# The second token half's residual steps behind the first half's first eight blocks of h2

## The chip, the cores and the metric

The kernel runs on one core of one Trainium2 chip. The metric is the device time in microseconds (us). The engines are TensorE (PE; its weight loads are listed as PEld), VectorE (DVE), ScalarE (ACT), GpSimd (POOL) and SyncE (SP, which issues most loads).

## What is computed

One layer of a diffusion backbone over 256 latent tokens of width 2048, with 256 context tokens. The mixer (attention and a recurrent branch) ends in an output projection; then, in the reference:

```python
out_l = merge_branches(attn_l, hgo_l, hg_l[6], gl_l, hgrn_o_norm[layer],
                       w_br_mla[layer], w_br_hgrn[layer], w_out[layer])
x = x + gt_a * rmsnorm(out_l, norm_g[layer, 1])
h = modulate(rmsnorm(x, norm_g[layer, 2]), sh_f, sc_f)
x = x + gt_f * rmsnorm(swiglu(h, w_ffn_in[layer], w_ffn_out[layer]), norm_g[layer, 3])
```

The change lies between the output projection (`w_out`) and the first products of the feed-forward part (`w_ffn_in`). Everything is float32; each large product is made of three passes over operands that are split into a high part and a low part (high x high, low x high, high x low).

## The kernel before

Tokens are in two halves of 128 (`hf` 0 and 1), the width of 2048 in four chunks of 512 (`c`) or 16 of 128 (`k`).

The output projection runs `project_tok` four times, for four column chunks, with both halves in two PSUM tiles. In the fourth, the last products are ordered so that half 0 ends 12 products before half 1. ACT squares each result with a sum (line 860), DVE multiplies it by the gate row into `x1` (863), and after the fourth chunk `rstd_part` makes the factor `r1[hf]` of the norm (838 to 840).

The residual steps follow, for half 0 and then for half 1 in program order: four times a DVE step that forms `x1 * r1 + xr` (line 871) and an ACT square with a sum (873), then `rstd_part` for `rt2[hf]`.

Then h2, the normed and modulated input of the feed-forward part, is made transposed. For every half and chunk, DVE forms `xq` = `x1` x `rt2` x `A2b` (881), PE transposes it in four pieces into one PSUM bank (884), and for each of the four pieces ACT writes the high part (888, with the shift as bias) and DVE the low part (889: the same value less the high part). There are four such PSUM banks (pool `px`), eight `xq` buffers. The instructions of the last piece are kept in `h2[hf, c]`.

The first chunk of the feed-forward products (`first_chunk`) takes its weights in pieces of 1024 columns, two `k` each. `half` splits one piece: an ACT cast makes the high part (line 108), DVE the low part (110). The split of `k` 0 to 3 (`wf0`) was made before, behind the output projection. `products` runs three matmuls for each `k` and half (919): first `k` 0 to 9 for half 0, then the same for half 1, then the rest with the halves in turn. The third matmul of each `k` is the one that needs the low part of the weights. The splits go through three pairs of buffers. `mod_job` is a DVE reduction over another loaded tile that shares the load buffers. After the first chunk, `project_tok` (825) does all further feed-forward products.

The program is queued by the Tile scheduler, which takes, for each engine, what is ready in its own model of the time, and among that what was written earlier first. `issue_after` adds only an order: the instructions of its block on an engine are queued behind the named instruction of the same engine. In the kernel before, such orders put the first split behind block (0, 0) of h2 and the second and third behind block (0, 1). The residual steps of half 1 have none.

Of the kernel before, what the change touches and what calls it, by code (L numbers as in the profile page):

```python
# [7 lines left out]
F32 = mybir.dt.float32  # L8
F32R = mybir.dt.float32r
U32 = mybir.dt.uint32  # L10
AF = mybir.ActivationFunctionType
ALU = mybir.AluOpType
PSUM = bass.MemoryType.PSUM

P = 128
# [4 lines left out]
NFF = 44  # L20
# [6 lines left out]
def block_kernel(  # L27
# [20 lines left out]
    nc = tc.nc  # L48
# [3 lines left out]
    ap = ctx.enter_context(tc.tile_pool(name="ap", bufs=16))  # L52
# [3 lines left out]
    px = ctx.enter_context(tc.tile_pool(name="px", bufs=4, space=PSUM))  # L56
# [17 lines left out]
    ident = c0[:, 0:128]  # L74
# [23 lines left out]
    def load_w(src, cols=2048):  # L98
        raw = wp.tile([P, cols], F32, tag="raw", name="raw")
        last_load[0] = nc.sync.dma_start(raw, src)  # L100
        return raw

    def split_w(raw, cols=2048, tags=("wH", "wL"), step=1024, pool=wp, bufs=None):
        parts = []
        for o in range(0, cols, step):
            n = min(step, cols - o)
            H = pool.tile([P, n], F32R, tag=tags[0], name="wH", bufs=bufs)
            nc.scalar.copy(H, raw[:, o:o + n])  # L108
            L = pool.tile([P, n], F32R, tag=tags[1], name="wL", bufs=bufs)
            nc.vector.tensor_tensor(L, raw[:, o:o + n], H.bitcast(F32), op=ALU.subtract)  # L110
            parts.append((H, L))

        def get(o, n):
            H, L = parts[o // step]
            q = o % step
            return H[:, q:q + n], L[:, q:q + n]

        return get

    def split_into(raw, tiles):  # L120

        for i, (H, L) in enumerate(tiles):
            nc.scalar.copy(H, raw[:, i * 512:(i + 1) * 512])
            nc.vector.tensor_tensor(L, raw[:, i * 512:(i + 1) * 512], H.bitcast(F32), op=ALU.subtract)

        def get(o, n):
            return tuple(t[:, o % 512:o % 512 + n] for t in tiles[o // 512])

        return get

    def split_act(dst, src, heng=None):
        nc.scalar.copy(dst[:, 0, :], src)
        nc.vector.tensor_tensor(dst[:, 1, :], src, dst[:, 0, :].bitcast(F32), op=ALU.subtract)
# [38 lines left out]
    def wide(u):  # L172
        return u.rearrange("p e t -> p (e t)")
# [93 lines left out]
    for g, nk in enumerate(GROUPS + [0, 0]):  # L267
# [6 lines left out]
        for kt in range(nt):  # L274
            if nk:
# [4 lines left out]
                for kk in range(per):  # L280
                    k = kt * per + kk
                    nc.tensor.matmul(pm[32 * (k % 4):32 * (k % 4) + 32, 0:n], cst[:, k], raw[:, kk * n:(kk + 1) * n],  # L282
                                     start=(k < 4), stop=(k >= KD - 4))
# [14 lines left out]
        pt = px.tile([P, 512], F32, tag="px", name="pt")  # L298
        for i in range(2 * nk):
            nc.tensor.matmul(pt[:, 2 * i:2 * i + 2], row[:, i * P:(i + 1) * P], sel,  # L300
                             start=(i == 0), stop=(i == 2 * nk - 1))
# [5 lines left out]
                                       op0=ALU.add, op1=ALU.mult)  # L307
# [441 lines left out]
    units = [hx[:, 1, 8 + j] for j in range(8)] + [hx[:, 0, j] for j in range(8)]  # L749
    spare = [hx[:, 1, j] for j in range(8)] + [hx[:, 0, 8 + j] for j in range(8)]  # L750
    for j in range(KD):
# [4 lines left out]
        for br, src in enumerate(([aT[:, h] for h in range(NH)], hgT)):  # L756
            for k in range(NH):
                H, L = w(br * 1024 + k * P, P)
                for z, (l, r) in enumerate(((H, src[k][:, 0, :]), (H, src[k][:, 1, :]), (L, src[k][:, 0, :]))):
                    nc.tensor.matmul(ps[:, br * T:(br + 1) * T], l, r, start=(br == 0 and k == 0 and z == 0),  # L760
                                     stop=(br == 1 and k == NH - 1 and z == 2))
# [15 lines left out]
    SH2 = wk.tile([P, KD], F32, name="SH2")  # L777
# [11 lines left out]
    def rows(i, vec, tiles):  # L789
        pg = px.tile([P, 512], F32, tag="px", name="pg")  # L790
        nc.tensor.transpose(pg[0:KD, 0:P], vec, ident)
        grow = wk.tile([KD, P], F32, tag="scs", name="grow")
        nc.scalar.copy(grow, pg[0:KD, 0:P])
        nc.sync.dma_start(gdr[i], grow)
        for c, g in enumerate(tiles):
            nc.sync.dma_start(g, gdr[i, 4 * c:4 * c + 4].rearrange("k p -> (k p)").partition_broadcast(P))
        return tiles
# [37 lines left out]
    def rstd_part(i, hf):  # L835

        rt = wk.tile([P, 16], F32, name=f"rt{i}{hf}")[:, 0:1]
        nc.vector.tensor_reduce(rt, ssq[:, i, hf], axis=mybir.AxisListType.X, op=ALU.add)
        nc.scalar.activation(rt, rt, AF.Sqrt, bias=epst, scale=1.0 / D)
        nc.vector.reciprocal(rt, rt)  # L840
        return rt

    def pairs(tiles):
        return list(zip(tiles[0::2], tiles[1::2]))

    g1b = gate_rows(0, [ap.tile([P, 512], F32, tag="hC", name="gbc", bufs=8) for _ in range(4)])
    x1 = bp.tile([P, 2, D], F32, tag="b16", name="x1")
# [3 lines left out]
    A2b = rows(2, A2, [wk.tile([P, 512], F32, tag=t, name="A2b") for t in ("kt", "ktn", "vT", "vn")])  # L851
# [12 lines left out]
        if c == 0:  # L864
            sqrt_table(ssq[:, 0, 0, 0:1])
    wf0 = split_into(load_w(wfi[0, 0]), pairs([wide(u) for u in spare[8:]]))
    rt2 = []
    for hf in range(2):
        for c in range(4):
            cs = slice(c * 512, (c + 1) * 512)  # L870
            nc.vector.scalar_tensor_tensor(x1[:, hf, cs], x1[:, hf, cs], r1[hf], xr[:, hf, cs], op0=ALU.mult, op1=ALU.add)
            junk = wk.tile([P, 512], F32, tag=("f", "kk")[hf], name="junk")
            nc.scalar.activation(junk, x1[:, hf, cs], AF.Square, accum_out=ssq[:, 1, hf, c:c + 1])
        rt2.append(rstd_part(1, hf))

    h2 = {}
    for hf in range(2):
        ts_ = slice(hf * P, (hf + 1) * P)
        for c in range(4):
            xq = ap.tile([P, 512], F32, tag="hC", name="xq", bufs=8)  # L880
            nc.vector.scalar_tensor_tensor(xq, x1[:, hf, c * 512:(c + 1) * 512], rt2[hf], A2b[c], op0=ALU.mult, op1=ALU.mult)
            pt = px.tile([P, 4, P], F32, tag="px", name="pxt")
            for i in range(4):
                nc.tensor.matmul(pt[:, i], xq[:, i * P:(i + 1) * P], ident, is_transpose=True, start=(i == 0), stop=(i == 3))
            for i in range(4):
                j = 4 * c + i
                h = units[j]
                hi = nc.scalar.activation(h[:, 0, ts_], pt[:, i], AF.Identity, bias=SH2[:, j:j + 1], scale=1.0)
                lo = nc.vector.scalar_tensor_tensor(h[:, 1, ts_], pt[:, i], SH2[:, j:j + 1], h[:, 0, ts_].bitcast(F32),
                                                    op0=ALU.add, op1=ALU.subtract)  # L890
            h2[hf, c] = (hi, lo)


    G = [None] * NFF
    g_row = []

    def behind(ins):
        es = ExitStack()
        for i in ins:
            es.enter_context(tc.issue_after(i.ins))  # L900
        return es

    def first_chunk():

        ps = [pj.tile([P, 512], F32, tag="pj", name="pst") for _ in range(2)]
        raws = [load_w(wfi[0, 1]), load_w(wfi[0, 2])]
        ws = [lambda k: wf0(k * 512, 512)] * 4

        def half(raw, i):
            w = split_w(raw[:, i * 1024:(i + 1) * 1024], 1024)  # L910
            for kk in range(2):
                ws.append(lambda k, kk=kk: w(kk * 512, 512))

        def products(ks, hf):
            for k in ks:
                H, L = ws[k](k)
                aH, aL = (units[k][:, e, hf * P:(hf + 1) * P] for e in range(2))
                for n, (l, r) in enumerate(((aH, H), (aL, H), (aH, L))):
                    nc.tensor.matmul(ps[hf], l, r, start=(k == 0 and n == 0), stop=(k == KD - 1 and n == 2))  # L919

        with behind(h2[0, 0]):
            half(raws[0], 0)
        with behind(h2[0, 1]):
            half(raws[0], 1)
            half(raws[1], 0)
        products(range(0, 10), 0)
        products(range(0, 10), 1)
        half(raws[1], 1)
        raw = load_w(wfi[0, 3])
        half(raw, 0)  # L930
        half(raw, 1)
        for k in range(10, KD):
            for hf in range(2):
                products((k,), hf)
        return ps
# [18 lines left out]
    def turn(j):  # L954

        g = g_row[2 * j:]
        for b in range(0, 4, 2):
# [5 lines left out]
            for i in range(2):  # L963
                G[4 * j + b + i] = u = spare[(4 * j + b + i) % 16]
                split_act(u, pt[:, i])
# [4 lines left out]
    def ffn_out(part, hook):  # L970
        q0 = 4 * part
        nq = min(4, NFF // 4 - q0)
        for c in range(4):
            cs = slice(c * 512, (c + 1) * 512)
            ps = project_tok(lambda q: wfo[c, q0 + q], 4 * nq, lambda k: G[4 * q0 + k], part == 0, part == 2,
                             pairs([ap.tile([P, 512], F32R, tag="hC", name="wl", bufs=8) for _ in range(8)])
# [168 lines left out]
```

## Time and profile before

| | |
|---|---|
| Median of 3 runs | 1741.63 us (1738.98 to 1741.84) |
| Profiled execution | 1740.55 us, span 1738.8 us |
| PE busy | 1694.0 us, 97% of the span |
| DVE busy | 1089.0 us, 63% |
| ACT busy | 766.2 us, 44% |
| Mean granted clock of PE | 0.991 |

Times in rows count from the start of the span. A busy PE is not a PE at its peak, since matmuls overlap; how closely their starts follow each other tells more. A timeline row merges neighbouring instructions of one kind: start, length of the whole, engine, line, operation, output <- inputs, shape, count, and in brackets the idle time before it and what ended it. The granted clock is a share of 2.4 GHz.

### The profile page before, as it was taken

Reading aid. Unit: us, or ns where it says so; the run is one execution under the profiler, and the core shown is the slowest. Engines: PE = TensorE matmul, PEld = TensorE weight load, DVE = VectorE, ACT = ScalarE, POOL = GpSimd, SP = SyncE. Lnnn points to the kernel's source line nnn. Section 1 sums busy time; section 2 is a strip of 40 time slices with the busy share of each in tenths; the row PEclk is TensorE's granted clock in tenths of the full one; section 3 lists DMA queues with packets and bytes.
Section 4 is the critical chain, followed back from the end, with each engine's and each line's share of the span. In section 5 each row is a group of like instructions: output and inputs, shape, how many; then the busy total and the mean of one; then the engine's idle time right before and its main releaser. Section 6 shows DMA issues by size and latency. Waiting matters only on the chain.

```text
span 1738.8 us, 22134 instructions
## 1 busy us (share of the span) xinstructions
PE 1694.0 (97%) x8715; PEld 1410.4 (81%) x8715; DVE 1089.0 (63%) x1619; ACT 766.2 (44%) x1086; POOL 51.7 (3%) x81
## 2 busy tenths in 40 slices
PE   6898999999999999999999899999999999999997
PEld 4457888888888888889998788888888888888886
DVE  5335777777778766666765765664456655544456
ACT  5225443343345444445544554444444443344443
POOL 0100000000000000001210000000000000000000
PEclk9899999999999999999999999999999999999999
DMA  9983455655556565578766456665566665555653
GB/s 389 357 330 148 162 178 194 217 194 194 180 183 231 193 253 189 194 290 303 278 222 224 167 218 242 234 234 187 194 242 233 234 233 208 194 193 185 214 193 121
DMA packets 60247, 383.78 MB, mean 221 GB/s; under 512 B 7104, under 2 KB 7920, under 8 KB 16880
## 3 DMA queue, kind: packets, MB, share of 16 engines
q1 hardware_dynamic: 55328, 368.15, 58.1%
q0 software_dynamic: 4096, 13.11, 1.9%
q8 instruction: 68, 1.11, 0.3%
q10 hardware_dynamic: 720, 1.12, 0.2%
q14 instruction: 35, 0.29, 0.0%
HBM read 376.03 MB, written 6.32 MB: 220 GB/s over the span
## 4 chain that ended last, share of the span: by engine, by line
PE 94%; DMA 2%; DVE 2%; ACT 1%; issue 0%; SPq 0%; DVEq 0%; ACTq 0%
PE pst L825 45%; PE ps L144 13%; PE ps L148 11%; PE ps L149 5%; PE psb L760 5%; PE pre L144 3%; DMA raw<-in_wm_dram 2%; PE pm L282 1%; PE pst L919 1%; PE psS L698 1%; PE po L722 1%; PE psS L695 1%; PE pv L670 1%; PE pq L654 1%; PE pk L144 1%; PE pgt L961 1%
## 5 line engine op out<-in xcount | busy, mean ns | idle before, releaser
L110 DVE TENSOR_TENSOR wL<-raw,wH 128x1024 fp32r<-128x1024 f32 x480 | 589.8, 1231 | 480.0 <-ACT wH L108 458.2
L108 ACT CAST wH<-raw 128x1024 fp32r<-128x1024 f32 x480 | 503.4, 1050 | 710.8 <-PE pst L825 393.1
L825 PE MATMUL pst<-wH,hx 128*128 128x512 f32 x2272 | 660.6, 390 | 0.0
L825 PEld LDWEIGHTS pst<-wH,hx 128*128 128x128 f32 x2272 | 425.6, 188 | 87.7
L825 PE MATMUL pst<-wL,hx 128*128 128x512 f32 x1136 | 402.2, 389 | 0.0
L148 PE MATMUL ps<-hx,wH 128*128 128x512 f32 x832 | 300.6, 402 | 2.8 <-DVE lat L367 2.8
L825 PEld LDWEIGHTS pst<-wL,hx 128*128 128x128 f32 x1136 | 213.2, 188 | 44.4
L149 PE MATMUL ps<-hx,wL 128*128 128x256 f32 x832 | 235.6, 284 | 0.0
L144 PE MATMUL ps<-hx,wH 128*128 128x512 f32 x672 | 212.5, 395 | 0.0
L148 PEld LDWEIGHTS ps<-hx,wH 128*128 128x128 f32 x832 | 156.9, 189 | 40.2 <-DVE lat L367 3.1
L346 DVE CUSTOM_DVE_ANT_0 raw<-raw,cb 128x2048 f32<-128x2048 f32 x64 | 146.1, 2283 | 31.8 <-DMA raw<-in_wm_dram 31.6
L149 PEld LDWEIGHTS ps<-hx,wL 128*128 128x128 f32 x832 | 157.7, 190 | 3.3 <-DVE mx L700 1.1
L144 PEld LDWEIGHTS ps<-hx,wH 128*128 128x128 f32 x672 | 125.0, 188 | 25.2
L144 PE MATMUL ps<-hx,wL 128*128 128x512 f32 x336 | 131.7, 392 | 0.0
L144 PEld LDWEIGHTS ps<-hx,wL 128*128 128x128 f32 x336 | 63.1, 188 | 12.8
L144 PE MATMUL pre<-hx,wH 128*128 128x512 f32 (+1 forms) x204 | 66.7, 410 | 5.4 <-ACT hx L201 5.3
L144 PEld LDWEIGHTS pre<-hx,wH 128*128 128x128 f32 x204 | 39.6, 204 | 25.6 <-ACT hx L201 10.8
L760 PE MATMUL psb<-hx,wH 128*128 128x256 f32 x256 | 46.8, 283 | 0.0
L760 PE MATMUL psb<-hC,wH 128*128 128x256 f32 x256 | 46.8, 283 | 0.0
L760 PEld LDWEIGHTS psb<-hx,wH 128*128 128x128 f32 x256 | 39.9, 192 | 0.0
L760 PEld LDWEIGHTS psb<-hC,wH 128*128 128x128 f32 x256 | 39.9, 192 | 0.0
L282 PE MATMUL pm<-raw,cst 128*32 128x512 f32 (+1 forms) x320 | 34.9, 538 | 4.3 <-DMA raw<-in_wm_dram 4.2
(256 smaller groups left out, 1416.8 us busy)
## 6 DMA issues: line engine op xcount, KB each, us to landing
raw<-in_wm_dram SPq DMA_DIRECT2D x96, 1024.0 KB, 4.9
raw<-in_wfi_dram SPq DMA_DIRECT2D x88, 1024.0 KB, 4.8
raw<-in_win_dram SPq DMA_DIRECT2D x73, 1024.0 KB, 4.8
raw<-in_wfo_dram SPq DMA_DIRECT2D x44, 1024.0 KB, 4.8
raw<-in_wbr_dram SPq DMA_DIRECT2D x16, 1024.0 KB, 5.6
raw<-in_wout_dram SPq DMA_DIRECT2D x16, 1024.0 KB, 4.9
raw<-in_wqk_dram SPq DMA_DIRECT2D x4, 1024.0 KB, 5.3
sgd<-sgx POOLq DMA_DIRECT2D x16, 256.0 KB, 5.0
```

Source lines behind the costliest of these rows:

```text
L108: nc.scalar.copy(H, raw[:, o:o + n])
L110: nc.vector.tensor_tensor(L, raw[:, o:o + n], H.bitcast(F32), op=ALU.subtract)
L144: nc.tensor.matmul(o, l, r, start=(first and i == 0), stop=(last and i == len(seq) - 1))
L148: nc.tensor.matmul(ps, w[0], act.rearrange("p e t -> p (e t)"), start=first, stop=False)
L149: nc.tensor.matmul(ps[:, 0:T], w[1], act[:, 0, :], start=False, stop=last)
L282: nc.tensor.matmul(pm[32 * (k % 4):32 * (k % 4) + 32, 0:n], cst[:, k], raw[:, kk * n:(kk + 1) * n], start=(k < 4), stop=(k >= KD - 4))
L346: nc.vector.tensor_tensor_reduce(out=raw, in0=raw, in1=cbt[0], scale=1.0, scalar=0.0, op0=ALU.mult, op1=ALU.add, accum_out=mod2[:, i // KD ...
L654: nc.tensor.matmul(pq[:, i * T:(i + 1) * T], l, r, start=(k == 0 and i == 0 and z == 0), stop=(k == 3 and i == 1 and z == 2))
L670: nc.tensor.matmul(pv[:, i, :], ckvs[:, k, l, ts_], r, start=(i == 0 and k == 0 and z == 0), stop=(i == 1 and k == 1 and z == 2))
L695: nc.tensor.matmul(psS, qn[a][:, i * T + qb * P:i * T + (qb + 1) * P], kn[b], start=(n == 0), stop=False)
L760: nc.tensor.matmul(ps[:, br * T:(br + 1) * T], l, r, start=(br == 0 and k == 0 and z == 0), stop=(br == 1 and k == NH - 1 and z == 2))
L825: mm = nc.tensor.matmul(ps[hf], l, r, start=(k == 0 and n == 0), stop=(k == nk - 1 and n == 2))
```

## The change

The residual steps become a function `residual(hf)` and the making of one block of h2 a function `second_norm(hf, c)`. Half 0's residual steps and its first two blocks of h2 (eight pieces of 128 columns) are written first, then half 1's residual steps, queued on ACT and DVE behind the last piece of block (0, 1), and then the other blocks. The first split of the first chunk moves from behind block (0, 0) to behind (0, 1), the second from (0, 1) to (0, 2), the third from (0, 1) to (0, 3). The number of instructions and their shapes stay.

```diff
-    rt2 = []
-    for hf in range(2):
+    h2 = {}
+    rt2 = {}
+
+    def residual(hf):
         for c in range(4):
             cs = slice(c * 512, (c + 1) * 512)
             nc.vector.scalar_tensor_tensor(x1[:, hf, cs], x1[:, hf, cs], r1[hf], xr[:, hf, cs], op0=ALU.mult, op1=ALU.add)
             junk = wk.tile([P, 512], F32, tag=("f", "kk")[hf], name="junk")
             nc.scalar.activation(junk, x1[:, hf, cs], AF.Square, accum_out=ssq[:, 1, hf, c:c + 1])
-        rt2.append(rstd_part(1, hf))
+        rt2[hf] = rstd_part(1, hf)
...
+    def second_norm(hf, c):
...
+    residual(0)
+    second_norm(0, 0)
+    second_norm(0, 1)
+    with behind(h2[0, 1]):
+        residual(1)
+    second_norm(0, 2)
+    second_norm(0, 3)
+    for c in range(4):
+        second_norm(1, c)
...
-        with behind(h2[0, 0]):
+        with behind(h2[0, 1]):
             half(raws[0], 0)
-        with behind(h2[0, 1]):
+        with behind(h2[0, 2]):
             half(raws[0], 1)
+        with behind(h2[0, 3]):
             half(raws[1], 0)
```

## Rows read from the trace of the kernel before

**Rows 1.** The page: PE in 40 slices (busy tenths), chain shares by engine.
```profile
PE   6898999999999999999999899999999999999997
PE 94%; DMA 2%; DVE 2%; ACT 1%; issue 0%; SPq 0%; DVEq 0%; ACTq 0%
```

**Rows 2.** Windows by stage: length, then busy PE, PEld, DVE, ACT, POOL, clock, DMA.
```profile
988.00:1001.00 13.00, 7.52 (x31) 5.83 (x31) 12.32 (x29) 9.16 (x28) 0.00 (x0) 0.74 0.00 1
1001.00:1022.00 21.00, 21.00 (x101) 17.36 (x100) 16.02 (x32) 14.14 (x28) 0.00 (x0) 1.00 0.55 201
1022.00:1062.00 40.00, 40.00 (x182) 33.24 (x181) 25.09 (x25) 17.57 (x20) 0.00 (x0) 1.00 0.63 229
```

**Rows 3.** Timeline of PE, 976 to 1030 us: start, length, instruction, count, idle before.
```profile
984.90 2.88 PE L825 MATMUL pst<-hx 128*128 128x512 f32 x12
990.21 1.32 PE L884 MATMUL pxt<-c,xq 128*128 128x128 f32 x8 [2.42 <-DVE xq L881]
991.32 0.49 PE L919 MATMUL pst<-hx 128*128 128x512 f32 x1
994.18 1.97 PE L884 MATMUL pxt<-c,xq 128*128 128x128 f32 x8 [2.37 <-DVE xq L881]
995.80 3.84 PE L919 MATMUL pst<-hx 128*128 128x512 f32 x9
1000.54 0.66 PE L884 MATMUL pxt<-c,xq 128*128 128x128 f32 x4 [0.90 <-DVE hx L889]
...
1001.96 0.39 PE L919 MATMUL pst<-wL,hx 128*128 128x512 f32 x1
...
1005.40 0.39 PE L919 MATMUL pst<-wL,hx 128*128 128x512 f32 x1
...
1021.76 0.39 PE L919 MATMUL pst<-wL,hx 128*128 128x512 f32 x1
```

**Rows 4.** Timeline of DVE in the same stretch.
```profile
989.40 1.42 DVE L881 SCALAR_TENSOR_TENSOR xq<-x,rt,A2b 128x512 f32<-128x512 f32 x2
990.73 2.73 DVE L871 SCALAR_TENSOR_TENSOR x<-x,rt,xr 128x512 f32<-128x512 f32 x4
993.38 1.41 DVE L881 SCALAR_TENSOR_TENSOR xq<-x,rt,A2b 128x512 f32<-128x512 f32 x2
994.71 0.60 DVE L889 SCALAR_TENSOR_TENSOR hx<-pxt,SH,hx 128x128 fp32r<-128x128 f32 x2
...
996.71 2.07 DVE L881 SCALAR_TENSOR_TENSOR xq<-x,rt,A2b 128x512 f32<-128x512 f32 x3
...
1000.40 1.22 DVE L110 TENSOR_TENSOR wL<-raw,wH 128x1024 fp32r<-128x1024 f32 x1
...
1002.30 2.36 DVE L110 TENSOR_TENSOR wL<-raw,wH 128x1024 fp32r<-128x1024 f32 x2
1004.57 2.17 DVE L889 SCALAR_TENSOR_TENSOR hx<-pxt,SH,hx 128x128 fp32r<-128x128 f32 x8
```

**Rows 5.** Timeline of ACT in the same stretch.
```profile
990.90 0.37 ACT L888 ACTIVATE hx<-pxt,SH 128x128 fp32r<-128x128 f32 x1 [1.87 <-PE pxt L884]
...
995.09 0.89 ACT L888 ACTIVATE hx<-pxt,SH 128x128 fp32r<-128x128 f32 x3 [0.28 <-DVE hx L889]
...
997.29 1.09 ACT L108 CAST wH<-raw 128x1024 fp32r<-128x1024 f32 x1
```

**Rows 6.** The chain that ended last, in order of time: start, length, what.
```profile
990.82 2.65 DVE x L871 x4
```

**Rows 7.** Timeline of SP, the load queue, 960 to 1040 us.
```profile
1010.81 12.51 SPq L100 DMA_DIRECT2D raw<-in_wfi_dram  x4
```

**Rows 8.** Windows of 2 us, columns as in rows 2.
```profile
992.00:994.00 2.00, 0.00 (x0) 0.00 (x0) 2.00 (x4) 1.94 (x6) 0.00 (x0) 0.57 0.00 0
996.00:998.00 2.00, 2.00 (x6) 1.60 (x6) 1.98 (x6) 2.00 (x7) 0.00 (x0) 0.50 0.01 4
```

More of the change, by code (lines that the diff above doesn't have):

```diff
@@ L873, in block_kernel @@
             nc.scalar.activation(junk, x1[:, hf, cs], AF.Square, accum_out=ssq[:, 1, hf, c:c + 1])
-        rt2.append(rstd_part(1, hf))
-    h2 = {}
-    for hf in range(2):
+        rt2[hf] = rstd_part(1, hf)
+    def second_norm(hf, c):
         ts_ = slice(hf * P, (hf + 1) * P)
[L879 to L895, printed above, removed]
+        xq = ap.tile([P, 512], F32, tag="hC", name="xq", bufs=8)
+        nc.vector.scalar_tensor_tensor(xq, x1[:, hf, c * 512:(c + 1) * 512], rt2[hf], A2b[c], op0=ALU.mult, op1=ALU.mult)
+        pt = px.tile([P, 4, P], F32, tag="px", name="pxt")
+        for i in range(4):
+            nc.tensor.matmul(pt[:, i], xq[:, i * P:(i + 1) * P], ident, is_transpose=True, start=(i == 0), stop=(i == 3))
+        for i in range(4):
+            j = 4 * c + i
+            h = units[j]
+            hi = nc.scalar.activation(h[:, 0, ts_], pt[:, i], AF.Identity, bias=SH2[:, j:j + 1], scale=1.0)
+            lo = nc.vector.scalar_tensor_tensor(h[:, 1, ts_], pt[:, i], SH2[:, j:j + 1], h[:, 0, ts_].bitcast(F32),
+                                                op0=ALU.add, op1=ALU.subtract)
+        h2[hf, c] = (hi, lo)
     def behind(ins):
@@ L901, in behind @@
         return es
+    residual(0)
[7 more added lines that the diff above has]
+        second_norm(1, c)
+    G = [None] * NFF
+    g_row = []
     def first_chunk():
```

## The prediction

> **What bounds the kernel now.** I began with the page: TensorE (PE) is busy in nine tenths or more of nearly every slice and carries 94% of the chain that ended last [rows 1]. So this change, all of whose edits lie in one short stage, counts only if PE comes out of that stage sooner. The windows by stage give the place: from 988 to 1001 us PE is busy 7.5 of 13 us while VectorE (DVE) is busy 12.3; from 1001 on, and in the stages behind, PE is busy all the time [rows 2]. The last product of the first chunk starts at 1021.76 [rows 3], and what follows is PE back to back. A microsecond won or lost before 1001.96 or in the rest of the first chunk is therefore a microsecond of the whole.
>
> Then PE's own timeline [rows 3]. After the output projection's last 12 products it waits 2.42 us for the first xq, transposes two blocks and does one product (991.32), waits again 2.37 us, transposes two blocks, does nine products in 3.84 us, and from 1000.54 on runs without a gap. DVE's timeline says why [rows 4]: xq of blocks 0 and 1 at 989.40, then at 990.73 the second half's four residual steps (2.73 us), then xq of blocks 2 and 3, and only at 994.71 the first low part of h2. ScalarE (ACT) had written the matching high part at 990.90, in 0.37 us [rows 5]: that low part could have run at about 991.3. The chain of waits has those four residual steps on it with 2.65 us [rows 6]. This is what the change takes away.
>
> I call the blocks of 512 columns 0.0 to 0.3 (first half) and 1.0 to 1.3; each has one xq, four transposes, four high parts (ACT) and four low parts (DVE). wL1, wL2, wL3 are the low parts of the weight splits that k = 4 to 9 need, 1024 columns each. k = 0 to 3 use a split made long before.
>
> **Unit prices from the rows.** Low parts behind each other: eight in 2.17 us, 0.26 each [rows 4]. Residual steps: four in 2.73, 0.66 each; xq: three in 2.07, 0.67 each. Splits on DVE: two in 2.36, 1.14 each. Within one block high and low alternate: the high part at 995.09 had waited for the low part at 994.71, so 0.38 from low to high [rows 4, 5], and about as much back (estimate from ACT's 0.37): 0.78 for a pair, 3.1 us for a block, with other blocks in the gaps. Products at full clock: 12 in 2.88 us, the last of them 0.39 long, so 0.227 each [rows 3]. From the third product of k = 4 (1001.96) to that of k = 8 (1005.40) PE did 12 products, 2.72 us, and one block's four transposes, which so cost 0.72.
>
> **The change part by part.** (1) Residual steps of the second half behind the last low part of block 0.1. On DVE xq of 0.2 and 0.3 now have nothing ahead of them and fill 990.73 to 992.07. The first low part comes at 991.4 (if it goes first) to 992.1, not 994.71. The last low part of block 0.1 is then issued between 994.4 (two blocks alternating alone, three pairs of 0.78 on) and 996.2 (all 16 low parts taking turns, 16 x 0.26). The residual steps follow, 2.66 us, and end at 997.4 to 998.9. Nothing waits behind them but the same DVE queue.
>
> (2) What is late next is k = 4. With low parts from 992 on PE does k = 0 to 3 (12 products, 2.7 us) by about 995.5; the third product of k = 4 needs wL1. In the kernel before wL1 ran at 1000.40 and PE passed that product at 1001.96 [rows 3, 4]. Now wL1 is queued behind block 0.1 on both engines; its cast (1.09 us, [rows 5]) runs while DVE does the residual steps, and that hides it. wL1 then runs at 997.4 at the earliest and at 1000 at the latest (behind what is left of blocks 0.2 and 0.3). I take 998.7, 1.7 us sooner, because 0.2 and 0.3 will have been partly done in the gaps of 0.0 and 0.1. Not all of this is gain: by 1001.96 the kernel before had also transposed block 1.0 (0.72), which is still to come. Gain here about 1.0, between -0.3 and 2.3.
>
> (3) Splits moved one or two blocks later (wL1 behind 0.1, wL2 behind 0.2, wL3 behind 0.3). By themselves they cost nothing: in the old order wL2 and wL3 ran at 1002.30, long after those low parts. What decides is DVE's sum. It had no idle time between 989.40 and the end of wL3 at 1004.66, in which it did 8 xq, 4 residual steps, 13 low parts and 3 splits (and the small steps of the norm). The new order needs, for the same point, 4 xq and 16 low parts: 4 x 0.67 less, 3 x 0.26 more, 1.9 us less; gaps of the high-low chain may give 0.5 back. So wL3 ends at 1003.3 if nothing of the second half goes ahead of it, at 1005.9 if the four xq do, and at 1010.1 if its 16 low parts do too (16 x 0.26). PE needs wL3 at the third product of k = 8, before at 1005.40 [rows 3]. With 1003.3 PE is there 2.05 sooner but with the transposes of 1.0 and 1.1 not yet done (1.44): gain 0.6. With 1005.9 it is 0.55 later, but the transposes of all four blocks are done by then where two had been: gain 0.9. So both middle cases give about the same.
>
> (4) The second half itself. From its first residual step to its first xq the old order took 990.73 to 996.71, 6.0 us [rows 4]. Starting at 994.7 to 996.5 its xq comes at 1000.7 to 1002.5. Its first low part follows in some 1.9 us (as 989.40 to 991.3 in the first half), 1002.6 to 1004.4. PE wants it after the 30 products of k = 0 to 9, not before 1003; cover for the early case, up to 1 us of wait for the late one. The residual steps issue no DMA. The loads on SP's queue wait for the splits that free their tiles; the next wave goes out from 1010.81 [rows 7], and its data are first multiplied after 1021.76, so a shift of a few microseconds is hidden by that distance. POOL has nothing here.
>
> The sum: these are two readings of one gain, 1.0 at wL1 and 0.6 to 0.9 at wL3; the later one decides, and I take its 0.9. The profiled execution took 1740.55 us (span 1738.8), so 1739.6; it lies 1.1 below the median of the runs shown, 1741.63, from which the same gain gives **1740.7 us**.
>
> **Clock.** From 992 to 998 the granted clock was 0.57 to 0.50, the 1.2 GHz level, after two gaps with little work between [rows 8], and the nine products at 995.80 took 0.43 each. They were not what the end waited for: DVE was. In the new order one gap is closed and another opens, from 995.5 to wL1 at about 999.9. The Trainium skill ("TensorE: Matmul & The Clock Gate", section "Why this matters for your kernels") warns that idle gaps between bursts put the engine back to half rate. By that rule products after the new gap would start slow where the old order had full clock from 1001 on; the trace shows the fall itself, not what this gap would do.
>
> **Rivals.** (a) Slower: the second half's low parts go ahead of wL2 and wL3. They stand before the splits in program order, and in the new order all four transpose buffers are free when 1.0 to 1.3 arrive, whereas in the old one block 1.0's transposes waited for a buffer until 1000.54. Price: wL3 at 1010.1, PE 4.75 late, less 1.44 for transposes done: 3.3 slower, 1744.9. It loses from about three such low parts on (0.9 / 0.26). Against it: the order before put wL2 and wL3 ahead of eight low parts [rows 4]. Chance 0.15.
> (b) Faster: wL1, wL2 and wL3 all fall into the time in which DVE would wait for the second half's norm (997.7 to 1001.1). Then PE has k = 0 to 9 done at about 1002, waits for the second half until 1003, and has 66 products and two blocks of transposes left, 15.0 + 1.4: the next chunk's first product at 1019.4, where it would have followed the last one at 1021.76 + 0.23, so 2.6 faster, 1739.0. Against it: three casts of 1.09 and four squares must share ACT in those 3.4 us. Chance 0.20.
> (c) The gap only moves, and PE resumes at 1.2 GHz: ten products at 0.43 instead of 0.23 cost 2.0 against the 0.9 won: 1.1 slower, 1742.7. For it: the fall in [rows 8]; against: PE has 12 products between the gaps where it had one. Chance 0.12.
> The forecast keeps 0.53.
>
> **Range and chances.** From (b) with 1.7 us more for the scatter of the runs shown (1738.98 to 1741.84) to (a): 1737.3 to 1744.9. 0.2% (3.5 us) is about what a measurement of this kernel can tell from no change. Faster by more than that needs (b) and some scatter on top: 0.15. Slower by more: (a) lies at that bound, so half of it, and the tail of (c): 0.12. Within: 0.73.
>
> **What would show it.** Right: low parts from about 992, the four residual steps at 995 to 996, wL1 near 998.7, first-chunk end near 1021. Step 2 is wrong if wL1 comes after 1000.4; step 3 if PE waits at k = 6 or 8 while DVE does low parts of the second half; step 4 if PE waits for 1.0. Wrong altogether if the order of work far behind the stage changes, or PE is no longer back to back there.

## The result and the profile after

The kernel after takes 1745.38 us (median of 8 runs, 1742.94 to 1747.07) against 1741.43 (8 runs, 1738.98 to 1743.09) for the kernel before: a ratio of 1.0022, 95% interval 1.0013 to 1.0031. It is 3.9 us slower. The prediction was 1740.7 us, with a range that ended at 1744.9.

One length is used from here on. **S** runs from the start of the last 12 products of the output projection (line 825, the last thing before the stage) to the first product behind the first chunk (line 825 again). Before, it is 984.90 to 1021.99 us, 37.09; after, 986.55 to 1027.18, 40.63. These 3.54 us are the loss: behind S, PE is back to back in both, and the rest of the span is the same (716.8 and 716.7 us). The output projection itself ended 1.65 us later in the profiled execution of after (runs of one kernel scatter by that much), so 1.65 is taken off wherever times of after are set beside the rows of before.

PE of the kernel after, from the last output products to the end of the first chunk (columns as in [rows 3]):

```profile
986.55 2.88 PE L825 MATMUL pst<-hx 128*128 128x512 f32 x12
991.85 1.32 PE L884 MATMUL pxt<-c,xq 128*128 128x128 f32 x8 [2.42 <-DVE xq L881]
...
994.25 3.19 PE L929 MATMUL pst<-hx 128*128 128x512 f32 x11
...
1000.75 0.50 PE L929 MATMUL pst<-wL,hx 128*128 128x512 f32 x1 [2.50 <-DVE wL L110]
...
1006.59 2.77 PE L884 MATMUL pxt<-c,xq 128*128 128x128 f32 x16
1009.11 0.48 PE L929 MATMUL pst<-wL,hx 128*128 128x512 f32 x1
...
1011.27 3.83 PE L929 MATMUL pst<-hx 128*128 128x512 f32 x11 [0.76 <-DVE hx L889]
...
1026.96 0.39 PE L929 MATMUL pst<-wL,hx 128*128 128x512 f32 x1
```

The change did what it was made for: the wait of 2.37 us for the third xq [rows 3] is gone, and k = 0 to 3 run at 994.25 instead of waiting. Up to 1000.75, the third product of k = 4, the kernel after is ahead: 999.10 with the 1.65 taken off, against 1001.96 [rows 3]. At the third product of k = 8 (1009.11, so 1007.46 against 1005.40) it is behind, and between there and the last product of the chunk it falls further back: 17.85 us against 16.36, although 8 transposes (two blocks) fewer, and one product more, are left to do.

DVE of the kernel after in the same stretch (columns as in [rows 4]):

```profile
991.05 2.74 DVE L881 SCALAR_TENSOR_TENSOR xq<-x,rt,A2b 128x512 f32<-128x512 f32 x4
...
994.48 2.43 DVE L889 SCALAR_TENSOR_TENSOR hx<-pxt,SH,hx 128x128 fp32r<-128x128 f32 x9 [0.18 <-ACT hx L888]
996.83 2.73 DVE L873 SCALAR_TENSOR_TENSOR x<-x,rt,xr 128x512 f32<-128x512 f32 x4
999.48 1.22 DVE L110 TENSOR_TENSOR wL<-raw,wH 128x1024 fp32r<-128x1024 f32 x1
...
1001.13 0.15 DVE L838 TENSOR_REDUCE rt<-ssq 128x1 f32<-128x4 f32 x1
...
1002.58 1.23 DVE L110 TENSOR_TENSOR wL<-raw,wH 128x1024 fp32r<-128x1024 f32 x1 [0.58 <-ACT wH L108]
1003.73 0.15 DVE L840 RECIPROCAL rt<-rt 128x1 f32<-128x1 f32 x1
...
1004.05 2.73 DVE L881 SCALAR_TENSOR_TENSOR xq<-x,rt,A2b 128x512 f32<-128x512 f32 x4
1006.69 1.22 DVE L110 TENSOR_TENSOR wL<-raw,wH 128x1024 fp32r<-128x1024 f32 x1
1008.65 2.29 DVE L346 CUSTOM_DVE_ANT_0 raw<-raw,cb 128x2048 f32<-128x2048 f32 x1 [0.74 <-DMA raw<-in_wm_dram]
...
1010.87 4.22 DVE L889 SCALAR_TENSOR_TENSOR hx<-pxt,SH,hx 128x128 fp32r<-128x128 f32 x16
```

Line 346 is the reduction of `mod_job`, work for a later part that nobody waits for here. It waits 0.74 us for its load and runs 2.29 us, and all 16 low parts of the second half stand behind it. Before, the same reduction ran at 1008.48 behind 23 of the 32 low parts, the eight of the last line of [rows 4] among them (DVE of the kernel before):

```profile
1008.48 2.29 DVE L346 CUSTOM_DVE_ANT_0 raw<-raw,cb 128x2048 f32<-128x2048 f32 x1 [0.95 <-DMA raw<-in_wm_dram]
```

The chain that ended last, of the kernel after, goes through that load and that reduction, where before it went through the residual steps [rows 6] and, from 1000.54 on, through PE alone:

```profile
1003.84 4.79 DMA raw<-in_wm_dram
...
1008.65 2.29 DVE raw L346
...
1010.95 3.38 DVE hx L889 x13
```

The last view is the granted clock in windows of 2 us, of the kernel after (columns as in [rows 2]; the clock is third from the end):

```profile
998.00:1000.00 2.00, 0.25 (x2) 0.00 (x0) 2.00 (x4) 1.94 (x6) 0.00 (x0) 1.00 0.04 8
1000.00:1002.00 2.00, 1.25 (x4) 0.67 (x4) 1.89 (x6) 1.83 (x7) 0.00 (x0) 0.88 0.01 4
1002.00:1004.00 2.00, 1.56 (x4) 0.64 (x3) 1.42 (x4) 1.94 (x4) 0.00 (x0) 0.50 0.00 0
...
1008.00:1010.00 2.00, 2.00 (x15) 1.86 (x14) 1.35 (x1) 1.15 (x4) 0.00 (x0) 0.92 0.00 0
```

The slow stretch of [rows 8] has moved from 992 to 998 (where PE had nine products to do and waited for DVE before and behind them) to 1002 to 1008, where PE has products to do. The 16 transposes take 2.77 us there.

### The profile page after: what moved, and what is told of

The parts are those of the page before. It is cut to its first block, busy times and chain, and to the rows that moved or that the text cites. A ratio compares the mean times of both kernels' runs of the same rounds, so it can differ in the third digit from the quotient of the medians.

```text
span 1743.9 us, 22130 instructions
## 1 busy us (share of the span) xinstructions
PE 1699.2 (97%) x8715; PEld 1409.7 (81%) x8715; DVE 1086.7 (62%) x1619; ACT 763.8 (44%) x1086; POOL 55.0 (3%) x81
## 4 chain that ended last, share of the span: by engine, by line
PE 93%; DVE 2%; DMA 2%; ACT 1%; issue 0%; SPq 0%; DVEq 0%; ACTq 0%
PE pst L825 45%; PE ps L144 13%; PE ps L148 11%; PE ps L149 5%; PE psb L760 5%; PE pre L144 4%; DMA raw<-in_wm_dram 1%; PE pm L282 1%; PE psS L698 1%; PE po L722 1%; PE pst L929 1%; PE psS L695 1%; PE pv L670 1%; PE pq L654 1%; PE pk L144 1%; DMA xt<-in_ctxT_dram 1%
```

## The experiments

Four explanations were set against each other. **M**: the mod reduction ahead of the second half's low parts. **C**: the 1.2 GHz stretch. **G**: the new places of the three splits. **L**: the second half's norm, which now begins late. Each kernel below is the kernel after but for its edits, except e6, which starts from the kernel before; where a heading names another kernel (e8 to e10: e7), the diff is against that one. `behind(x)` puts the order of `issue_after` on each instruction of `x`, and `ExitStack()` puts none: only the first reduction of the feed-forward part is moved. Ratios are to the kernel before on the same chip, S is from the profiled execution.

| kernel | splits | residual steps of half 1 | reduction | S, us | ratio (95% interval) |
|---|---|---|---|---|---|
| before | old | old | free | 37.09 | 1 |
| after | new | new | free | 40.63 | 1.0022 (1.0013 to 1.0031) |
| e1 | new | new | behind 1.3 | 38.54 | 1.0003 (0.9995 to 1.0012) |
| e2 | new | new, PE kept busy | behind 1.3 | 37.60 | 1.0001 (0.9992 to 1.0010) |
| e3 | old | new | free | 40.79 | 1.0019 (1.0011 to 1.0028) |
| e4 | old | new | behind 1.3 | 37.55 | 1.0001 (0.9993 to 1.0010) |
| e5 | new | old | free | 37.68 | 1.0003 (0.9994 to 1.0012) |
| e6 | old | old | behind 1.3 | 37.08 | 1.0000 (0.9991 to 1.0009) |
| e7 | early | new | behind 1.3 | 35.07 | 0.9989 (0.9981 to 0.9998) |
| e8 | early | ahead of all xq | behind 1.3 | 37.70 | 0.9998 (0.9990 to 1.0007) |
| e9 | early | old | behind 1.3 | 37.87 | 0.9999 (0.9990 to 1.0008) |
| e10 | early | new | free | 37.29 | 1.0004 (0.9995 to 1.0012) |
| e11 | new | new, PE kept busy | free | 39.89 | 1.0014 (1.0006 to 1.0023) |

The ratios tell e7 (faster), after, e3 and e11 (slower) from the kernel before; among the others it is S that tells them apart, and S of one profiled execution. How far S scatters was not measured; the nearest thing to a repeat is e6 against the kernel before, 0.01 us apart.

**e1: the reduction behind the last low part of block 1.3.**

```diff
-            mod_job(1)
+            with behind(h2[1, 3]) if j == 0 and i == 0 else ExitStack():
+                mod_job(1)
```

> The changed kernel with one order added: the reduction over the first w_mod tile (line 346 of it, 2.29 us on DVE) is queued behind the last low part of h2. Stage length means here: from the start of the last 12 products of the output projection to the first product of line 825 behind the first chunk: 37.1 us in the kernel before (984.90 to 1021.99), 40.6 in the changed one (986.55 to 1027.18). Theory M (the reduction, which ran from 1008.65 to 1010.95 ahead of all low parts of the second half, holds PE): these low parts start at about 1008.1, PE meets them at 1010.1 without a wait, 66 products of 0.227 remain, so 2.1 us shorter: stage 38.5, about 1743.3. Theory C (PE at 1.2 GHz from 1001 to 1008 is what cost the time) and theory L (the second half's norm is late, the reduction only fills a wait): no change beyond 0.5, 1745.

S is 38.54, M's number, and 2.09 shorter than in the kernel after. PE and DVE of e1:

```profile
1005.63 2.75 PE L884 MATMUL pxt<-c,xq 128*128 128x128 f32 x16
...
1009.15 2.91 PE L929 MATMUL pst<-hx 128*128 128x512 f32 x12
```

```profile
1007.13 0.35 DVE L889 SCALAR_TENSOR_TENSOR hx<-pxt,SH,hx 128x128 fp32r<-128x128 f32 x1 [0.17 <-ACT hx L888]
...
1012.38 2.28 DVE L346 CUSTOM_DVE_ANT_0 raw<-raw,cb 128x2048 f32<-128x2048 f32 x1
```

The second half's low parts start at 1007.13, and PE does its 12 products without a wait, in 2.91 us instead of the 3.83 of 11 after. The reduction runs later and nobody misses it. The transposes still take 2.75 us: the slow stretch is untouched.

**e2: e1, and PE kept busy in its gap** by twelve products into a spare tile, between the second and the third product of k = 4.

```diff
+                    if (k, hf, n) == (4, 0, 2):
+                        last = mm
+                        idle = pj.tile([P, 512], F32, tag="pj", name="pst")
+                        for z in range(12):
+                            with tc.issue_after(last.ins):
+                                last = nc.tensor.matmul(idle, units[0][:, 0, 0:P], wf0(0, 512)[0],
+                                                        start=(z == 0), stop=(z == 12 - 1))
...
-                    nc.tensor.matmul(ps[hf], l, r, start=(k == 0 and n == 0), stop=(k == KD - 1 and n == 2))
+                    mm = nc.tensor.matmul(ps[hf], l, r, start=(k == 0 and n == 0), stop=(k == KD - 1 and n == 2))
```

> As e1, and 12 extra products into a tile nobody reads (the first k's operands again) are put on PE behind the second product of k = 4, to fill the 3 us in which it waits for wL1 and keep its clock up. Theory C: PE stays at 2.4 GHz through 1001 to 1008, and the third product of k = 8, which came at 1009.1 behind 16 transposes at half clock, comes when wL3 is ready, about 1007.9: 1.2 us shorter than e1, stage 37.3. If the clock is not restored, or theory M alone holds: as e1 or, where the extra products do not fit the gap, up to 0.5 longer.

S is 37.60, 0.94 under e1. PE of e2, and the clock window in which the transposes lie:

```profile
994.58 2.88 PE L934 MATMUL pst<-hx 128*128 128x512 f32 x12
...
1001.88 1.47 PE L884 MATMUL pxt<-c,xq 128*128 128x128 f32 x12
```

```profile
1002.00:1004.00 2.00, 2.00 (x18) 1.69 (x16) 2.00 (x3) 1.10 (x3) 0.00 (x0) 1.00 0.94 393
```

The extra products fill the time in which PE waited for wL1; the clock stays at 1.00 (in each window from 994 to 1006), and 12 transposes take 1.47 us where 16 took 2.75. C is right in kind and came out 0.3 us smaller than expected. PE still waits 0.64, 0.53 and 0.46 us for the second cast, wL2 and wL3.

**e3: the splits back in their old places**, the reduction left free.

```diff
-        with behind(h2[0, 1]):
+        with behind(h2[0, 0]):
             half(raws[0], 0)
-        with behind(h2[0, 2]):
+        with behind(h2[0, 1]):
             half(raws[0], 1)
-        with behind(h2[0, 3]):
             half(raws[1], 0)
```

> The changed kernel with the three split orders put back (first split behind block 0.0, second and third behind block 0.1); the second half's residual steps stay behind block 0.1. Theory G (the moved splits did it: wL1 and wL2 late, wL2 ahead of the norm's reciprocal): wL1 runs ahead of the residual steps, PE does k = 4 to 9 without the 2.5 us gap, and the time returns to the kernel before or below: stage 36 to 37. Theory M: the reduction is still ahead of the second half's low parts; it starts when its load has landed, some 1.6 us sooner than in the changed kernel because wL2 frees the load tile sooner: stage 39.0, about 1743.8.

S is 40.79. G as the whole cause falls: with the old places the loss is as large as in the kernel after. M's figure was missed by 1.8 us. PE and DVE of e3:

```profile
1008.47 4.68 PE L929 MATMUL pst<-hx 128*128 128x512 f32 x11 [1.82 <-DVE hx L889]
```

```profile
1005.86 2.29 DVE L346 CUSTOM_DVE_ANT_0 raw<-raw,cb 128x2048 f32<-128x2048 f32 x1
...
1008.07 4.22 DVE L889 SCALAR_TENSOR_TENSOR hx<-pxt,SH,hx 128x128 fp32r<-128x128 f32 x16
```

The reduction is again ahead of the low parts. PE waits 1.82 us for it, and the 11 products behind that wait take 4.68 us: in this kernel the clock fell there (0.50 from 1010 to 1012 us). So here M brought its own C with it.

**e4: e3 and e1 together.**

```diff
-        with behind(h2[0, 1]):
+        with behind(h2[0, 0]):
             half(raws[0], 0)
...
-            mod_job(1)
+            with behind(h2[1, 3]) if j == 0 and i == 0 else ExitStack():
+                mod_job(1)
```

> e3 with the order of e1 as well. Theory M with G's half: the second half's low parts start at about 1006.5 in the changed kernel's time, 66 products and the last transposes follow: stage 35.9 to 36.5, 1 us faster than the kernel before, 1740.5. If M is wrong: as e3.

S is 37.55: the reduction's place is worth 3.24 us here, and its slow stretch is gone with it. That is M again, but S missed the expected 35.9 to 36.5, for a reason in PE's rows of e4:

```profile
1001.28 0.50 PE L929 MATMUL pst<-wL,hx 128*128 128x512 f32 x1 [2.38 <-DVE wL L110]
...
1004.58 1.32 PE L884 MATMUL pxt<-c,xq 128*128 128x128 f32 x8 [0.70 <-DVE xq L881]
```

With the old places wL1 is early, and the wait that the change took from xq reappears at wL2, which now queues behind the residual steps: 2.38 us against the 2.37 of [rows 3].

Against e1 (38.54) the old places are worth 0.99 us where the reduction is out of the way, about what the twelve products gave in e2 (0.94), and the clock stayed at 1.00 in e2 and e4. So G is not nothing: the wait for wL1 in its new place is the one behind which the clock fell, and C came with it.

**e5: only the splits moved**, the residual steps in their old place.

```diff
+    residual(1)
     second_norm(0, 0)
     second_norm(0, 1)
-    with behind(h2[0, 1]):
-        residual(1)
     second_norm(0, 2)
```

> The kernel after with the second half's residual steps put back ahead of the first half's xq blocks; the three weight splits keep their new places behind blocks 0.1, 0.2 and 0.3, and the mod reduction is left free. S is the time from the start of the last 12 out-projection products to the first product behind the first chunk: 37.09 before, 40.63 after. In the order of the instructions wL1 now stands behind 12 of the first half's low parts instead of 6, wL2 behind 14 and wL3 behind 17, and the mod reduction behind 26. If the new places of the splits are what costs (theory G), the third product of k=4 comes some 1.6 us later than before (six low parts of 0.27 us) and S is 38.5 to 39.5. If the moved residual steps are what costs, with the mod reduction that they let past (M), S goes back to 37.1 or under.

S is 37.68, 0.59 over the kernel before and less than G's 1.4 to 2.4. Moved alone, the splits cost little: wL1 starts 16.69 us into S (before 15.50), and PE waits 0.31 for it. The reduction stands far enough back in this order that it costs nothing.

**e6: e1's edit in the kernel before.**

```diff
-            mod_job(1)
+            with behind(h2[1, 3]) if j == 0 and i == 0 else ExitStack():
+                mod_job(1)
```

> The kernel before with one edit, the same as in the first experiment: the first mod reduction goes behind block 1.3. Theory M says that the reduction costs only where it stands ahead of the second half's low parts that PE waits for; before it stood behind 23 of the 32, and PE had those it needed. So S stays at 37.1 within 0.3 and the ratio is 1.000. A rival, that the reduction costs about 2 us wherever it stands among the low parts, gives S 35.0 to 35.5.

S is 37.08 against 37.09. Before, the reduction was free: what the change did was to move the low parts past it, or it past them.

**e7: the three splits tied to nothing**, with the reduction behind block 1.3.

```diff
-        with behind(h2[0, 1]):
-            half(raws[0], 0)
-        with behind(h2[0, 2]):
-            half(raws[0], 1)
-        with behind(h2[0, 3]):
-            half(raws[1], 0)
+        half(raws[0], 0)
+        half(raws[0], 1)
+        half(raws[1], 0)
...
-            mod_job(1)
+            with behind(h2[1, 3]) if j == 0 and i == 0 else ExitStack():
+                mod_job(1)
```

> The kernel after with the three splits of the first half's weights no longer tied to any block (they then go ahead of the first half's normalisation, into a stretch in which DVE and ACT stand idle for 4 us while PE ends the output projection), and the mod reduction behind block 1.3. The residual steps keep the change's place behind block 0.1. If what the change loses is what queues between the low parts (splits and mod, theories G and M together), no product of k=4 to 9 waits for a weight, the clock does not fall, the first half's 30 products end 10 us after their xq, PE then waits 1 to 2 us for the second half's first low part (the residual steps and the norm behind them are late by the change), and S is 34.3 to 35.8: 1739 to 1740 us in all, under the kernel before. If the late second norm itself is what costs (theory L), PE waits there for 3 us and more and S stays at 37 or above.

S is 35.07, as expected if only what queues between the low parts costs, and the kernel is faster than both: 0.9989 of the kernel before, interval 0.9981 to 0.9998. DVE and PE of e7:

```profile
988.39 2.36 DVE L110 TENSOR_TENSOR wL<-raw,wH 128x1024 fp32r<-128x1024 f32 x2
...
1001.69 0.16 DVE L838 TENSOR_REDUCE rt<-ssq 128x1 f32<-128x4 f32 x1 [0.61 <-ACT junk L875]
...
1002.47 0.15 DVE L840 RECIPROCAL rt<-rt 128x1 f32<-128x1 f32 x1
1002.66 1.42 DVE L881 SCALAR_TENSOR_TENSOR xq<-x,rt,A2b 128x512 f32<-128x512 f32 x2
1003.99 0.35 DVE L889 SCALAR_TENSOR_TENSOR hx<-pxt,SH,hx 128x128 fp32r<-128x128 f32 x1
```

```profile
992.85 2.19 PE L884 MATMUL pxt<-c,xq 128*128 128x128 f32 x12 [3.29 <-DVE xq L881]
...
1003.56 1.23 PE L884 MATMUL pxt<-c,xq 128*128 128x128 f32 x8
1004.61 0.49 PE L929 MATMUL pst<-hx 128*128 128x512 f32 x1
...
1006.12 3.50 PE L929 MATMUL pst<-hx 128*128 128x512 f32 x11
```

The splits are done by 990.7; two of them delay the first half's norm, so PE's first wait grows from 2.42 to 3.29 us. From there on the timeline lists no wait of PE. The expected wait of 1 to 2 us for the second half did not come: its norm takes 0.78 us from reduce to reciprocal (2.60 after, where ACT's casts and wL2 stood in between), and the first low part follows the first xq in 1.33 us. L falls: a late second norm is harmless if nothing is queued into it. One thing that was expected failed: the clock did fall, to 0.62 and 0.53 in the windows from 994 to 998 us, behind the first wait.

**e8: e7 with the residual steps back in front.**

```diff
+    residual(1)
     second_norm(0, 0)
     second_norm(0, 1)
-    with behind(h2[0, 1]):
-        residual(1)
     second_norm(0, 2)
```

> As the kernel with early splits, but with the residual steps back in the old place ahead of the first half's xq blocks. This tells what the change's own idea is worth when no split and no mod reduction is in the way. In the instruction order the four residual steps (2.74 us) now stand ahead of all of the first half's xq, so PE starts 2.7 us later and does not wait for the second half at all. If the idea is worth something by itself, S is 0.5 to 1.5 longer than in the kernel with early splits, 35.5 to 36.5. If the second half's late norm eats it (theory L), S is the same or shorter.

S is 37.70, 2.63 over e7 where 0.5 to 1.5 was expected. PE starts 2.4 us later and then waits a second time, 1.78 us, for low parts behind the second half's four xq. It is no fair partner, since all four residual steps went ahead of all xq.

**e9: e7 with the residual steps where they were before**, between the second and the third xq.

```diff
-    with behind(h2[0, 1]):
+    with behind([xq_ins[0, 1]]):
         residual(1)
```

(`xq_ins` keeps the instruction of line 881 for each block.)

> The kernel with early splits and the mod reduction behind block 1.3, and the residual steps of the second half tied to the second xq of the first half, where the kernel before had them (two xq, four residual steps, two xq). It is the fair partner of the kernel with early splits (S 35.07), since the partner run before stood all four residual steps ahead of every xq (S 37.70). If the change's own move, the residual steps behind block 0.1, saves PE the wait of 2.4 us for the third xq and the one of 0.8 us behind the second half's xq, S is 37.5 to 38.0 here. If it only shifts the wait, S is 35.0 to 35.5.

S is 37.87. PE of e9 shows both waits that the change removes:

```profile
995.73 1.97 PE L885 MATMUL pxt<-c,xq 128*128 128x128 f32 x8 [2.36 <-DVE xq L882]
...
1002.08 0.66 PE L885 MATMUL pxt<-c,xq 128*128 128x128 f32 x4 [1.06 <-DVE hx L890]
```

So the change's own idea, the residual steps behind block 0.1, is worth 2.80 us (37.87 to 35.07) where nothing else queues in the way. The clock was low for a while in both (0.50 from 994 to 1000 us in e9); its part in the 2.80 was not separated.

The move and the early splits pay only together. With the old places the move makes S longer by 0.47 us (e6 to e4), and the early splits alone, with the residual steps in their old place, make it longer by 0.79 (e6 to e9): PE's first wait is 3.29 us in e9 too.

**e10: e7 with the reduction left free.**

```diff
-            with behind(h2[1, 3]) if j == 0 and i == 0 else ExitStack():
-                mod_job(1)
+            mod_job(1)
```

> The kernel with early splits, with the mod reduction left free. Its weight tile comes free early, so in the instruction order the reduction now stands between the first half's last xq and the first half's first low part. Theory M in its general form (2.29 us of an in-order queue ahead of low parts that PE waits for come out as 2.1 to 2.4 us of the stage, wherever that is) gives S 37.1 to 37.6 against 35.07 with the reduction behind block 1.3. If only the second half's low parts are exposed, S is 35.0 to 35.4.

S is 37.29, 2.22 over e7. The tile of its load now comes free so early that the reduction slips in ahead of the first half's low parts. DVE and PE of e10:

```profile
993.67 2.28 DVE L346 CUSTOM_DVE_ANT_0 raw<-raw,cb 128x2048 f32<-128x2048 f32 x1
```

```profile
996.28 4.63 PE L929 MATMUL pst<-hx 128*128 128x512 f32 x11 [1.80 <-DVE hx L889]
```

Wherever those 2.29 us stood ahead of low parts that PE wanted, S was longer by nearly all of them: 2.09 (e1 to after), 2.22 (e7 to e10, with the clock at 0.50 for a while in e10 as well) and 3.24 (e4 to e3, where in e3 alone the clock fell too).

**e11: the extra products of e2 alone**, the reduction left where the change put it.

```diff
+                    if (k, hf, n) == (4, 0, 2):
+                        last = mm
...
```

> The kernel after with twelve extra products on PE into a spare tile between the second and the third product of k=4, as in the second experiment, but with the mod reduction left where it was, ahead of the second half's low parts. If the clock's 0.94 us add to the reduction's 2.09 (C and M separate), S is 39.7 against 40.63 in the kernel after. If PE's slow stretch is hidden under the wait for the reduction (its load lands at the same time whatever PE does), S is 40.3 to 40.7.

S is 39.89, 0.74 under the kernel after, at a clock of 1.00 from 988 to 1014 us: C's part is there without e1's edit too. The reduction ran behind three of the second half's low parts here and ahead of the other 13. PE of e11 still waits for the low parts behind the reduction:

```profile
1007.65 2.80 PE L939 MATMUL pst<-hx 128*128 128x512 f32 x8 [1.70 <-DVE hx L889]
```

## Why the prediction was wrong, point by point

**The account.** Of the 3.54 us, the reduction's place is 2.09 (e1; 2.29 by e11 to e2), the slow clock 0.94 (e2; 0.74 by e11), together 3.03. The 0.51 left (e2 against before) is a net figure, with the wait that the change removed in it; it was not taken apart by a run. e2 shows PE waiting 0.64, 0.53 and 0.46 us for a cast and two splits there, and e7, in which no split is in the way, has none of these waits. A gain of 0.9 was forecast, so even without M and C the sum was off by 1.4 us: that is step 3.

**What bounds the kernel** was read rightly: PE is back to back behind the stage, and the change of S is the change of the time.

**Step 1 was right.** The low parts began at 993.71 (992.06 with the 1.65 off; said: 991.4 to 992.1), the last one of block 0.1 and those behind it ended at 996.9 (995.3; said: 994.4 to 996.2), and the residual steps at 999.56 (997.9; said: 997.4 to 998.9).

**Step 2 was right, on the safe side.** wL1 ran at 999.48 (997.83; said: 998.7, at the earliest 997.4), and k = 4's third product came 2.86 us sooner, 2.1 with the 0.72 for a block's transposes off (2.4 with the 0.49 of step 3): the upper end of what was given.

**Step 3 was right on DVE and wrong on PE.** wL3 ended at 1007.91 (1006.26), 0.4 beyond the middle case of 1005.9 in which the four xq go ahead. The norm was longer than before, which fits the excess: 2.60 us from reduce to reciprocal against 1.04, because its square root stood behind a cast on ACT and its reciprocal behind wL2 on DVE. The gain of 0.9 written beside that case did not come. In the kernel after, k = 8's third product came at 1007.46 instead of 1005.95: when wL3 was ready, PE was still at the 16 transposes in front of it, which took 2.77 us at 1.2 GHz.

The price of the transposes was wrong too. Between 1001.96 and 1005.40 the kernel before did 13 products, not 12; one is the second half's first (PE of the kernel before):

```profile
1003.34 0.60 PE L884 MATMUL pxt<-c,xq 128*128 128x128 f32 x4
1003.69 0.48 PE L919 MATMUL pst<-hx 128*128 128x512 f32 x1
```

With 13 x 0.227 off, 0.49 us is left for a block's transposes, not 0.72, and 0.98 for the two blocks that were put at 1.44. e2 tests the sum without the reduction and at full clock. There the product that waits for wL3 (PE of e2, S from 983.06)

```profile
1004.48 0.50 PE L939 MATMUL pst<-wL,hx 128*128 128x512 f32 x1 [0.46 <-DVE wL L110]
```

comes 0.92 us later in S than before, where 0.55 was said, and what follows it is shorter by 0.41, where 1.44 was said: 0.51 lost instead of 0.9 won. The wrong price explains 0.46 of the missing 1.03; for the rest the runs give no cause.

**Step 4 is the one that failed most.** The second half's first xq came at 1004.05 (1002.40), inside the 1000.7 to 1002.5 given. But "its first low part follows in some 1.9 us" became 6.82 us: on DVE all four xq (2.73), wL3 (1.22), the wait for the reduction's load (0.74) and the reduction (2.29) stood between (neighbouring rows overlap a little). The working listed only xq, residual steps, low parts and splits as DVE's work; the reduction, 2.29 us a few lines further down the same timeline, was in no sum because before it cost nothing (e6). The same paragraph looked at SP's loads from 1010.81 on [rows 7] and called a shift harmless. The one that mattered was the load before it, which brings the reduction's data. SP of the kernel after:

```profile
1003.84 0.33 SPq L100 DMA_DIRECT2D raw<-in_wm_dram  x1
1010.98 16.12 SPq L100 DMA_DIRECT2D raw<-in_wfi_dram  x4
```

It goes out when wL2 frees its tile, by the 1.65 at 1002.19, where before it went out at 1003.56. The split, and with it the load, came sooner, the second half's low parts came later, and the two crossed in the queue's order. That order is the Tile scheduler's, made by its own model of the time; that the earlier load is what moved the reduction ahead fits e10, where the load goes out at 988.62 and the reduction stands ahead of the first half's low parts as well, but was not tested by itself.

**The rivals.** (a) gave 1744.9, nearly the measured time, but by another mechanism: no low part of the second half ran ahead of wL2 or wL3. (b) happened in part and turned against itself: wL1 and wL2 did fall into the time of the second half's norm, and lengthened it. (c) happened as described, the gap moved and PE resumed at 1.2 GHz; its price was put at 2.0 and was 0.74 to 0.94, probably since part of those products waited for DVE anyway (PE still waits for wL2 and wL3 in e2). It was set down as a case of its own, with a chance of 0.12; in truth it came on top of M, which no rival named. The Trainium skill ("TensorE: Matmul & The Clock Gate", section "Why this matters for your kernels") warns that idle gaps between bursts bring the engine to half rate. The trace of the kernel after agrees, with 0.50 from 1002 to 1008 behind the wait of 2.50 us; in e4 a wait of 2.38 us left the clock at 1.00.

## What to carry to other kernels

When a piece of work is delayed on an in-order queue, list everything that is queued on that engine within the delay, also what cost nothing before: background work with no consumer nearby can pass ahead of the delayed work and cost nearly its full length (2.29 us of reduction, 2.09 to 2.22 of the stage). Tie such work explicitly behind what the bottleneck waits for, and put small prerequisites (here three splits, 1.2 us each) into an earlier idle stretch rather than one block later. With both, the reordering that lost 3.5 us wins 2 (e7); early splits without it lost 0.8 (e6 to e9), so such moves have to be tried together.

## What the hardware showed that was not expected

Gaps of nearly the same length on PE had different consequences. In the kernel after a wait of 2.50 us, behind 6 us of products and transposes, was followed by a clock of 0.50 for some 6 us; in e4 a wait of 2.38 us at nearly the same place, behind waits of 2.42 and 0.53, left the clock at 1.00; what decides between the two was not shown:

```profile
1002.00:1004.00 2.00, 1.88 (x9) 1.18 (x7) 1.85 (x8) 1.15 (x4) 0.00 (x0) 1.00 0.78 246
```

(The clock window of e4 behind that wait, columns as in [rows 2]; 996 to 1008 is at 1.00 in each window.) Twelve idle products, 2.88 us of PE that nobody else wanted, kept it at 1.00 in e2 and e11, and were worth 0.74 to 0.94 us.
